# Compressed-branch products of a sparse-attention layer: float32 column tiles in place of full-width split products

## The chip, the cores and the metric

The kernel runs on one core of a Trainium2 chip. The metric is the device time of one execution in microseconds (us). The engines are named as in the profile: PE is the matrix engine (TensorE) and PEld its weight loads, DVE is VectorE, ACT is ScalarE, POOL is GpSimd, and SP issues most DMAs. A name such as L709 is line 709 of the kernel before the change.

## The reference

Two layers on a sequence of 256 tokens of width 1024. Each layer is an adaptive RMS norm, a token mixer, and a gated residual; a final RMS norm follows. Layer 0 is sparse attention with three branches, layer 1 a chunkwise mLSTM. The change lies in layer 0's compressed branch. There, 16 heads in 4 groups (head dimension 64) attend to 15 compressed tokens, made from overlapping blocks of 32 tokens by a small network:

```python
k_cmp = compress_tokens(kv[:, :, 0], ...)      # gelu(flat @ w1 + b1) @ w2 + b2
v_cmp = compress_tokens(kv[:, :, 1], ...)
s_cmp = einsum('bsghd,bcgd->bghsc', q, k_cmp) * scale - slopes * dist_c
p_cmp = masked_probs(s_cmp, dist_c >= 0)
o_cmp = einsum('bghsc,bcgd->bsghd', p_cmp, v_cmp)
...
o = gates[:, :, 0] * o_cmp + gates[:, :, 1] * o_slc + gates[:, :, 2] * o_win
y = o.reshape(B, S, A_WIDTH) * silu(z)
return y @ w_out
```

With 256 tokens the selected and the sliding branch see all earlier keys, so both are plain causal attention over 256 keys of their own.

## The kernel before

**Precision.** Most products are made from split operands: a float32 matrix is written as a rounded part (type float32r, written by ACT, `make_hi`, L165) and the rest (written by DVE, `make_lo`, L170), and three products hi·hi, hi·lo and lo·hi are added up in PSUM. Some smaller products use plain float32 operands. The trace records a float32r product as one matmul and a float32 product as two, each with its weight load.

**Weights.** SP streams blocks of weights of up to 512 KB into ten raw buffers (`_load_one`, L88). A block's successor is loaded when its buffer is released by the split or by the product that reads it raw. Split blocks lie in six pairs of buffers `wh`, `wl`.

**Order.** In layer 0 (`first_phase`, `nsa`, `boundary`) the order of PE, ACT, DVE and SP is the order of the program text, under a manual schedule. In layer 1 of the reference (`layer2` in the code) a planner orders the instructions by its own model of their times, except for a few that are pinned.

**The stretch around the change**, in the program's order, with the names that the steps below use:

- `S(n)` for n = 0 to 7 makes the scores of the selected and the sliding branch for head i = n // 2 of two groups (L959, L963, in PSUM banks 0 to 2); DVE adds the position term and reduces to the minimum (L973); `softmax(n)` is the exp on ACT (L985); `factors(n)` and `scaled(n, j)` scale the probabilities on DVE (L993 to L995, L1002); `T_pair(n, j)` transposes them on PE (L1015, banks 5 and 6) and copies them out on ACT (L1017); `PV(n)` multiplies by the values (L1036, 64-column tiles, bank 7, which it keeps from PV(2i) to PV(2i + 1)).
- `z_steps(n)` are the split products of the gate path (L1662 to L1664, bank 4), in steps of three matmuls; `z_tanh` (ACT, L913) and `z_out` (DVE, L917) read the bank.
- The compressed tokens' second network layer makes `kb` (L679 for the keys, L681 for the values) in bank 3. From it DVE makes `kc` (L683), its rounded part `KcH` (L688) and its rest `KcL` (L689), and the values `Vc` (L694, four instructions). `KcH` and `KcL` have 160 columns for each group, of which 16 hold keys; POOL zeroes the rest (L686, L687). A slice of 128 columns at column 128·g of the flattened tile holds group g's keys at columns 32·g to 32·g + 15, since 160 = 128 + 32, and zeros elsewhere.
- `cmp_scores(i2)` (L709) makes the compressed scores of heads 2·i2 and 2·i2 + 1 in bank 3. Each of its 16 products has 128 columns of weights; the products of the four groups, of KcH and KcL, are added up into one bank half of all 128 partitions, where the zeros keep the groups apart. `Q` holds the rounded part of a query in one half of the partitions and its rest in the other. ACT copies the bank out (L710).
- The program then goes on with S(2), `factors(1)`, `scaled(1, 0)`, the second `cmp_scores`, `scaled(1, 1)`, `softmax` of S(2)'s first half, PV(0), the transposes of the scores `St` (`cmp_tokens(0)`: L724 on PE in bank 3, L725 on DVE), `T_pair(1, 0)`, `cmp_tokens(1)`, a split (L165, L170), and the compressed branch's softmax on DVE and ACT (L738 to L754), interleaved with `z_steps(1)`, S(3) and `T_pair(1, 1)`. Its probabilities come back transposed as `PcT` (L764, L765).
- `compressed(gp)`, at the end of every PV with odd n, adds the compressed branch to bank 7 with two float32 products of 128-column weights (L1028).
- `gate_steps(0, 4)` (float32 products of 32-column tiles, L227) follow in bank 4, after `z_out(1)` has read it.

Of the kernel before, what the change touches and what calls it, by code (L numbers as in the profile page):

```python
# [7 lines left out]
F32 = mybir.dt.float32  # L8
F32R = mybir.dt.float32r
# [3 lines left out]
OP = mybir.AluOpType  # L13
AX = mybir.AxisListType

P = 128
SEQ = 256
# [6 lines left out]
class Kernel:  # L24
# [526 lines left out]
    def nsa(self, acc):  # L551
        nc, t, p1, pc, ident = self.nc, self.t, self.p1, self.pc, self.ident
# [5 lines left out]
        Q = self.Q = []  # L558
# [105 lines left out]
        b = self.bank(3)  # L664
# [9 lines left out]
        self.T_pair(0, 1)  # L674
        self.go(z, 12)
        self.softmax(1)
        kb = self.bank(3)
        for k in range(2):
            nc.tensor.matmul(kb[:, 0:64], self.w2k[:, k].rearrange("p a d -> p (a d)"), hk[:, k], start=(k == 0), stop=(k == 1))  # L679
        for k in range(2):  # L680
            nc.tensor.matmul(kb[:, 64:128], hv[:, k].rearrange("p g s -> p (g s)"), self.w2v[:, k], start=(k == 0), stop=(k == 1), skip_group_check=True)  # L681
        kc = self.T(p1, [P, 4, 16])
        nc.vector.tensor_scalar(kc.rearrange("p g s -> p (g s)"), kb[:, 0:64], 0.5, self.pca[:, 88:89], op0=OP.mult, op1=OP.add)  # L683
        KcH = self.T(p1, [P, 4, 160], F32R, tag="tz", bufs=2)
        KcL = self.T(p1, [P, 4, 160], F32R, tag="tz", bufs=2)
        nc.gpsimd.memset(KcH.bitcast(F32), 0.0)  # L686
        nc.gpsimd.memset(KcL.bitcast(F32), 0.0)  # L687
        nc.vector.tensor_copy(KcH[:, :, 0:16], kc)  # L688
        nc.vector.tensor_sub(KcL[:, :, 0:16], kc, KcH[:, :, 0:16].bitcast(F32))  # L689
        Vc = self.Vc = self.T(p1, [P, 4, 64])  # L690
        nc.gpsimd.memset(Vc, 0.0)
        for g in range(4):
# [5 lines left out]


        St = [self.T(p1, [P, 2, SEQ], tag="y32", bufs=2) for _ in range(2)]  # L700
        KcHf = KcH.rearrange("p g x -> p (g x)")
        KcLf = KcL.rearrange("p g x -> p (g x)")

        def cmp_scores(i2):
            b = self.bank(3)
            for i in (2 * i2, 2 * i2 + 1):
                for g in range(4):
                    for n, kf in enumerate((KcHf, KcLf)):
                        nc.tensor.matmul(b[:, (i % 2) * SEQ : (i % 2) * SEQ + SEQ], kf[:, g * P : g * P + P], Q[i][:, g], start=(g == 0 and n == 0), stop=(g == 3 and n == 1))  # L709
            nc.scalar.activation(St[i2].rearrange("p i k -> p (i k)"), b, AF.Copy)  # L710

        cmp_scores(0)
        self.S(2)
        self.factors(1)
        self.scaled(1, 0)
        cmp_scores(1)
        self.scaled(1, 1)
        self.softmax(2, (0,))
# [300 lines left out]
    def PV(self, n):  # L1019

        nc = self.nc
        i, gp = n // 2, n % 2
        if gp == 0:
            self.ob = self.bank(7)
        o = self.ob[:, gp * SEQ : gp * SEQ + SEQ]

        def compressed(gp):
            nc.tensor.matmul(self.ob[:, gp * SEQ : gp * SEQ + SEQ], self.Vc[:, 2 * gp : 2 * gp + 2].rearrange("p g d -> p (g d)"), self.PcT[:, i], start=False, stop=True, skip_group_check=True)  # L1028

        for br in range(2):  # L1030
            for k in range(2):
                for j in range(2):
                    g = 2 * gp + j
                    oo = o[64 * j : 64 * j + 64, P * k : SEQ]
                    rhs = self.PT[n, j, br][:, 0:256] if k == 0 else self.PT[n, j, br][:, 256:384]
                    nc.tensor.matmul(oo, self.V[br][:, k, 64 * g : 64 * g + 64], rhs, start=(gp == br == k == 0), stop=False, skip_group_check=True, tile_position=(0, 64 * j))  # L1036
        if gp:
            for n in range(2):
                compressed(n)
# [666 lines left out]
```

## Time and profile before

| what | us |
|---|---|
| runs of the kernel before | 457.91, 459.12, 459.18 (median 459.12) |
| profiled execution: span from first to last instruction | 458.1 |
| PE busy | 444.2 (97% of the span) |
| DVE busy | 330.1 (72%) |
| ACT busy | 268.7 (59%) |
| the two `cmp_scores` groups (L709), from the first start | 106.7 to 108.7 and 110.1 to 112.1 |
| `compressed` groups (L1028), first starts | 125.0, 142.1, 165.2, 186.1 |

The profile gives no time of its execution beside the span. The granted clock of PE is 0.995 over the span. DMA moves 95.63 MB at a mean of 209 GB/s; from 103 to 114 us nearly nothing is moved, since all raw buffers are full.

How to read it: "start, length, what" are the first columns of a timeline or chain row; in a timeline a bracket at the end gives the idle time ahead of the row and what ended it. In the chain of waits a row's length is only what it adds to the chain. In a table of waits the numbers are the sum in us, how many times, and the longest. Matmuls are pipelined, so the next one starts before the one ahead of it ends: 0.12 us from start to start for 256 columns, with 0.28 us for each.

### The profile page before, as it was taken

What the parts mean: (1) busy time and instruction counts of PE and PEld (TensorE: products, weight loads), DVE (VectorE), ACT (ScalarE), POOL (GpSimd) and SP (SyncE); (2) the same over time, 40 slices, a digit from 0 to 9 for tenths busy, and PEclk for the clock granted to TensorE, in tenths of its full rate; (3) what the DMA queues carried; (4) which work ended last, traced back from release to release, by engine and by line L of the source; (5) the groups of instructions that cost most, each with busy time, mean ns of one, the idle gap of its engine ahead of it and who ended that gap; (6) DMA issues with size and microseconds to landing.
All of it is one profiled execution on the core that took longest, in us unless ns stands there. A gap on an engine that the chain in (4) does not pass through costs nothing.

```text
span 458.1 us, 8507 instructions
## 1 busy us (share of the span) xinstructions
PE 444.2 (97%) x3120; PEld 377.7 (82%) x3120; DVE 330.1 (72%) x777; ACT 268.7 (59%) x527; POOL 34.8 (8%) x101
## 2 busy tenths in 40 slices
PE   8899999999999999999999999999999999999993
PEld 3799898788948777778899889988888888888883
DVE  3655578886868867587998369688986978455745
ACT  4543377683678777456956686546745556454523
POOL 8820012100000000012000000000000000000000
PEclk9999999999999999999999999999999999999997
DMA  8999999991368899899899998897836699840002
GB/s 275 336 308 296 333 360 292 276 340 48 92 183 279 260 226 298 261 201 172 217 179 110 92 308 286 168 168 225 263 120 221 187 186 280 257 151 1 0 0 92
DMA packets 77596, 95.63 MB, mean 209 GB/s; under 512 B 4540, under 2 KB 56052, under 8 KB 77556
## 3 DMA queue, kind: packets, MB, share of 16 engines
q1 hardware_dynamic: 75828, 92.73, 76.4%
q0 software_dynamic: 1392, 1.58, 1.7%
q10 hardware_dynamic: 336, 0.80, 0.5%
q8 instruction: 24, 0.39, 0.4%
q14 instruction: 16, 0.13, 0.1%
HBM read 93.00 MB, written 1.05 MB: 205 GB/s over the span
## 4 chain that ended last, share of the span: by engine, by line
PE 80%; DMA 7%; DVE 6%; ACT 3%; SPq 3%; issue 1%; ACTq 0%; DVEq 0%
PE bank L547 9%; PE bank L549 9%; PE bank L548 9%; PE bank L1153 8%; PE bank L461 5%; PE bank L870 5%; PE bank L1663 5%; PE bank L1662 5%; PE bank L1664 5%; PE bank L1267 4%; PE bank L227 3%; SPq L88 3%; DMA raw<-in_a_w_in 3%; DMA Q<-in_ada_w 2%; DMA KH<-in_ada_w 2%; PE bank L1036 2%
## 5 line engine op out<-in xcount | busy, mean ns | idle before, releaser
L165 ACT ACTIVATE wh<-raw 128x1024 fp32r<-128x1024 f32 (+5 forms) x126 | 120.9, 977 | 95.1 <-PE bank L549 25.3
L170 DVE TENSOR_TENSOR wl<-raw,wh 128x1024 fp32r<-128x1024 f32 (+5 forms) x126 | 139.7, 1122 | 48.4 <-ACT wh L165 47.6
L547 PE MATMUL bank<-wh,one 128*128 128x512 f32 (+2 forms) x208 | 77.0, 371 | 0.0
L548 PE MATMUL bank<-wl,one 128*128 128x512 f32 (+2 forms) x208 | 76.4, 367 | 0.0
L549 PE MATMUL bank<-wh,one 128*128 128x512 f32 (+2 forms) x208 | 76.3, 368 | 0.0
L1662 PE MATMUL bank<-one,wh 128*128 128x256 f32 x208 | 59.7, 287 | 0.0
L1663 PE MATMUL bank<-one,wh 128*128 128x256 f32 x208 | 59.1, 284 | 0.0
L1664 PE MATMUL bank<-one,wl 128*128 128x256 f32 x208 | 59.1, 284 | 0.0
L547 PEld LDWEIGHTS bank<-wh,one 128*128 128x128 f32 x208 | 39.2, 189 | 7.0 <-issue 0.8
L549 PEld LDWEIGHTS bank<-wh,one 128*128 128x128 f32 x208 | 39.2, 188 | 6.1
L548 PEld LDWEIGHTS bank<-wl,one 128*128 128x128 f32 x208 | 39.2, 189 | 5.9
L1662 PEld LDWEIGHTS bank<-one,wh 128*128 128x128 f32 x208 | 39.8, 191 | 0.7 <-issue 0.4
L1663 PEld LDWEIGHTS bank<-one,wh 128*128 128x128 f32 x208 | 39.8, 192 | 0.1
L1664 PEld LDWEIGHTS bank<-one,wl 128*128 128x128 f32 x208 | 39.8, 191 | 0.0
L461 PE MATMUL bank<-one,wh 128*128 128x256 f32 x224 | 31.5, 286 | 0.2 <-ACT one L425 0.2
L985 ACT ACTIVATE Pr<-Pr,mn 128x128 f32<-128x128 f32 (+1 forms) x64 | 28.2, 448 | 2.4 <-DVE mn L973 2.4
L461 PEld LDWEIGHTS bank<-one,wh 128*128 128x128 f32 x224 | 28.5, 191 | 0.7 <-ACT one L425 0.5
L1153 PE MATMUL bank<-wl,QK 128*128 128x512 f32 (+1 forms) x80 | 28.2, 353 | 0.0
L1153 PE MATMUL bank<-wh,V 128*128 128x512 f32 (+1 forms) x80 | 28.0, 350 | 0.1
L1153 PE MATMUL bank<-wh,QK 128*128 128x512 f32 (+1 forms) x80 | 28.0, 350 | 0.0
L973 DVE CUSTOM_DVE_ANT_0 Pr<-bank,one 128x128 f32<-128x128 f32 (+1 forms) x64 | 18.4, 352 | 5.8 <-PE bank L959 5.7
L1481 DVE SCALAR_TENSOR_TENSOR conv<-bank,one,conv 128x255 f32<-128x255 f32 (+2 forms) x48 | 20.2, 470 | 2.1 <-ACT conv L1476 2.1
(325 smaller groups left out, 769.6 us busy)
## 6 DMA issues: line engine op xcount, KB each, us to landing
raw<-in_b_w_in SPq DMA_DIRECT2D x62, 512.0 KB, 8.3
raw<-in_ada_w SPq DMA_DIRECT2D x34, 512.0 KB, 5.8
raw<-in_b_w_out SPq DMA_DIRECT2D x16, 512.0 KB, 6.4
raw<-in_a_w_in SPq DMA_DIRECT2D x12, 512.0 KB, 7.6
Q<-in_ada_w SPq DMA_DIRECT2D x8, 512.0 KB, 8.2
raw<-in_a_cmp_w SPq DMA_DIRECT2D x8, 512.0 KB, 9.0
raw<-in_a_w_in SPq DMA_DIRECT2D x16, 256.0 KB, 4.2
raw<-in_a_w_out SPq DMA_DIRECT2D x16, 256.0 KB, 5.4
```

What stands on the lines that cost most here:

```text
L165: self.nc.scalar.activation(v(hi), src, AF.Copy)
L170: self.nc.vector.tensor_sub(v(lo), src, v(hi).bitcast(F32))
L461: nc.tensor.matmul(out, w[:, ch * P : ch * P + P], h[:, kk], start=(kk == 0 and m == 0 and ch % 2 == 0), stop=(kk == 7 and m == 2), skip_g ...
L547: nc.tensor.matmul(out, self.hh[:, kk, sl], wh, start=first, stop=False, skip_group_check=True)
L548: nc.tensor.matmul(out, self.hh[:, kk, sl], wl, start=False, stop=False, skip_group_check=True)
L549: nc.tensor.matmul(out, self.hl[:, kk, sl], wh, start=False, stop=last, skip_group_check=True)
L870: nc.tensor.matmul(out, l[:, sl], w[:, c0:c1], start=(k == 0 and m == 0), stop=(k == 7 and m == 2), skip_group_check=True)
L985: self.nc.scalar.activation(v, v, AF.Exp, bias=mn[:, a, br, j : j + 1], scale=-1.0, accum_out=sm[:, a, br, j : j + 1])
L1153: ins = nc.tensor.matmul(out, l[:, sl], w[:, c0:c1], start=(k == 0 and m == 0), stop=(k == N - 1 and m == 2), skip_group_check=True)
L1662: nc.tensor.matmul(out, wh, self.hh[:, kk], start=first, stop=False, skip_group_check=skip)
L1663: nc.tensor.matmul(out, wh, self.hl[:, kk], start=False, stop=False, skip_group_check=skip)
L1664: nc.tensor.matmul(out, wl, self.hh[:, kk], start=False, stop=last, skip_group_check=skip)
```

## The change

Three edits in layer 0.

1. `kb` is made in bank 7 instead of bank 3.
2. `KcH` and `KcL` go. `kc` gets 32 columns for each group, of which DVE writes 16 directly and POOL zeroes all 32 beforehand. A compressed score is now one float32 product for each group and head, with 32 columns of weights, at column tile 32·g of the array; it writes its own 32 partitions of the bank. A call has 8 products instead of 16.
3. `compressed(gp)` makes two float32 products of 64-column weights, one in each column half, instead of one of 128 columns.

```diff
-        kb = self.bank(3)
+        kb = self.bank(7)
...
-        kc = self.T(p1, [P, 4, 16])
-        nc.vector.tensor_scalar(kc.rearrange("p g s -> p (g s)"), kb[:, 0:64], 0.5, self.pca[:, 88:89], op0=OP.mult, op1=OP.add)
-        KcH = self.T(p1, [P, 4, 160], F32R, tag="tz", bufs=2)
-        KcL = self.T(p1, [P, 4, 160], F32R, tag="tz", bufs=2)
-        nc.gpsimd.memset(KcH.bitcast(F32), 0.0)
-        nc.gpsimd.memset(KcL.bitcast(F32), 0.0)
-        nc.vector.tensor_copy(KcH[:, :, 0:16], kc)
-        nc.vector.tensor_sub(KcL[:, :, 0:16], kc, KcH[:, :, 0:16].bitcast(F32))
+        kc = self.T(p1, [P, 4, 32])
+        nc.gpsimd.memset(kc, 0.0)
+        nc.vector.tensor_scalar(kc[:, :, 0:16], kb[:, 0:64].rearrange("p (g s) -> p g s", g=4), 0.5, self.pca[:, 88:89], op0=OP.mult, op1=OP.add)
...
         def cmp_scores(i2):
             b = self.bank(3)
             for i in (2 * i2, 2 * i2 + 1):
                 for g in range(4):
-                    for n, kf in enumerate((KcHf, KcLf)):
-                        nc.tensor.matmul(b[:, (i % 2) * SEQ : (i % 2) * SEQ + SEQ], kf[:, g * P : g * P + P], Q[i][:, g], start=(g == 0 and n == 0), stop=(g == 3 and n == 1))
+                    nc.tensor.matmul(b[32 * g : 32 * g + 32, (i % 2) * SEQ : (i % 2) * SEQ + SEQ], kc[:, g], Q[i][:, g].bitcast(F32), start=True, stop=True, tile_position=(0, 32 * g))
...
         def compressed(gp):
-            nc.tensor.matmul(self.ob[:, gp * SEQ : gp * SEQ + SEQ], self.Vc[:, 2 * gp : 2 * gp + 2].rearrange("p g d -> p (g d)"), self.PcT[:, i], start=False, stop=True, skip_group_check=True)
+            for j in range(2):
+                nc.tensor.matmul(self.ob[64 * j : 64 * j + 64, gp * SEQ : gp * SEQ + SEQ], self.Vc[:, 2 * gp + j], self.PcT[:, i], start=False, stop=True, skip_group_check=True, tile_position=(0, 64 * j))
```

More of the change, by code (lines that the diff above doesn't have):

```diff
@@ L700, in nsa @@
         St = [self.T(p1, [P, 2, SEQ], tag="y32", bufs=2) for _ in range(2)]
-        KcHf = KcH.rearrange("p g x -> p (g x)")
-        KcLf = KcL.rearrange("p g x -> p (g x)")
         def cmp_scores(i2):
```

## The prediction

> **What bounds the kernel now.** I read the page's span and busy shares first, then the busy time by stretches, then PE's waits behind 100 us, and last the chain of waits around the changed lines.
>
> ```profile
> span 458.1 us, 8507 instructions
> PE 444.2 (97%) x3120; PEld 377.7 (82%) x3120; DVE 330.1 (72%) x777; ACT 268.7 (59%) x527; POOL 34.8 (8%) x101
> ```
> ```profile
> core 0: us, PE busy (x) PEld busy (x) DVE busy (x) ACT busy (x) POOL busy (x), PEclk, DMA share, GB/s
> 115.10:127.50 12.40, 12.13 (x103) 10.90 (x101) 11.20 (x41) 8.54 (x28) 0.00 (x0) 1.00 0.29 86
> 137.50:441.00 303.50, 303.45 (x1889) 260.25 (x1890) 227.80 (x475) 184.49 (x332) 4.79 (x16) 1.00 0.78 193
> ```
> ```profile
> PE bank L930 <- ACT adaA L927: 0.7, 1, 0.7
> PE bank L709 <- DVE one L694: 0.5, 1, 0.5
> PE bank L227 <- DVE xT L917: 0.3, 1, 0.3
> ```
>
> PE is the bound: from 137.5 to 441 us it is busy for 303.45 of 303.50 us at clock 1.00. After 100 us only three waits are put down to another engine's work, and two of them lie near the change: L709, the compressed scores, waits 0.5 us for DVE, and L227 waits 0.3 us for L917. The stretch around the change in order of time:
>
> ```profile
> 105.21 0.21 DVE tz L688
> ...
> 105.51 0.23 DVE tz L689
> ...
> 106.33 0.24 DVE one L694
> ...
> 106.71 2.15 PE bank L709 x16
> ...
> 110.27 1.90 PE bank L709 x16
> 112.17 1.45 PE bank L1036 x16
> ...
> 114.21 0.34 PE bank L1015 x3
> ...
> 126.83 0.61 DVE xT L917
> ...
> 127.48 1.92 PE bank L227 x16
> ```
>
> Up to 114.5 us the chain is PE with the two L709 groups in it (2.15 + 1.90); from there to 127.4 it is almost all DVE, which is busy for 11.20 of the 12.40 us from 115.1 to 127.5 (the row above); then PE and, until 137.5, ACT. A shortening in front of 114 us must therefore also move DVE to be worth anything at 127.5.
>
> **The change part by part.** The sum is made against this execution's span of 458.1 us. The page gives no other time for it; the three runs are 457.91, 459.12 and 459.18, so the median stands 1.0 us above the span.
>
> *The bank.* The next rows are of the timelines of PE, DVE and ACT.
>
> ```profile
> 105.98 0.28 PE L1664 MATMUL bank<-one,wl 128*128 128x256 f32 x1
> 106.71 2.15 PE L709 MATMUL bank<-Q,tz 128*128 128x256 f32 x16 [0.45 <-DVE one L694]
> 108.70 0.28 PE L959 MATMUL bank<-KH,Q 128*128 128x256 f32 x1
> ```
> ```profile
> 104.82 0.28 DVE L683 TENSOR_SCALAR one<-bank,one 128x64 f32<-128x64 f32 x1 [1.79 <-PE bank L681]
> 106.92 0.69 DVE L917 SCALAR_TENSOR_TENSOR xT<-zb,bank 128x512 f32<-128x512 f32 x1 [0.36 <-ACT zb L913]
> 109.38 0.29 DVE L973 CUSTOM_DVE_ANT_0 Pr<-bank,one 128x128 f32<-128x128 f32 x1 [1.77 <-PE bank L959]
> ```
> ```profile
> 97.32 0.57 ACT L654 ACTIVATE one<-bank 128x512 f32<-128x512 f32 x1
> ```
>
> The first scores call waits for L694 only because both use bank 3: L694 is the last reader of the products kb. With kb in bank 7 it needs kc alone, ready at 105.10 (104.82 + 0.28). L1664 starts at 105.98 and the z matmuls stand 0.12 apart, so PE goes on at 106.10 and not at 106.71: 0.61 us on PE's path. Bank 7 is free for kb: its previous content is copied out by ACT L654 at 97.32 + 0.57, about 6 us earlier. Its next user, PV(0), comes at 109.5 by the working below, L694 is done 0.44 earlier than now (106.57), at 106.1, so 3.4 us of cover. The removed L688 and L689 (0.44 us) lie on DVE ahead of L694 and of L917, but L917 waits for ACT L913 anyway, so the change on DVE is worth 0 there. If PE were late, they would be worth their 0.4.
>
> *POOL.* Two memsets of 640 columns go, one of 128 columns comes, into a new tile that waits for no reader. They ran at 81.5 and 82.4, more than 20 us ahead of use:
>
> ```profile
> 81.52 0.63 POOL L686 MEMSET tz<- 128x640 f32 x1 [3.74 <-DVE PT L527]
> ```
>
> Nothing waits for them; 0 us. No DMA is added or removed, and no queue of SP or POOL is passed.
>
> *The scores.* Two calls, each 16 fp32r products of 256 columns with 128-column weights, start to next start 1.99 us (106.71 to 108.70). After it each call is 8 float32 products into four 32-column tiles, which the trace records as 16 matmuls, since a float32 product leaves two records. This form stands in L227 (rows of the chain: 128, 128 and 256 columns):
>
> ```profile
> 22.71 0.64 PE bank L227 x16
> ...
> 28.79 1.01 PE bank L227 x32
> ...
> 149.64 1.86 PE bank L227 x32
> ```
>
> The 32 records of 256 columns between full-width work took 1.86 us, so 16 take 0.93 at least. At 128 columns 16 cost 0.64 and 32 cost 1.01; going from 128 to 256 columns adds 0.85 per 32, so 0.43 per 16: 0.64 + 0.43 = 1.07 at most. I take 1.0 from the middle; each call loses 0.99 on PE. The fixed part of these rows (0.27 at zero records) includes the turn between whole array and tiles. The Trainium skill, TensorEngine Tiling (Array Packing), Key Properties, says that changing the tiling mode drains the engine; that speaks against the change, which adds such turns. The rows agree with a small price; without it a call would be 0.85 and the gain 0.15 per call more, with it it is the 1.0 taken.
>
> *What the shortening is worth.* S(2) moves from 108.70 to 107.10 (0.61 + 0.99 = 1.60 earlier), and its first DVE reduction, 0.68 behind it, to 107.78, behind L917's end at 107.61. So DVE gains 1.60. PE then has the second call 0.99 shorter and reaches the transposes of St and T_pair(1,0) 2.6 earlier. There it meets DVE:
>
> ```profile
> 112.25 1.93 DVE L1002 TENSOR_SCALAR Pr<-Pr,f 128x128 f32<-128x128 f32 x8
> 114.25 0.42 DVE L725 TENSOR_TENSOR tz<-bank,one 128x256 f32<-128x256 f32 x1
> 115.42 0.42 DVE L725 TENSOR_TENSOR tz<-bank,one 128x256 f32<-128x256 f32 x1 [0.75 <-PE bank L724]
> 116.11 1.29 DVE L170 TENSOR_TENSOR wl<-raw,wh 128x512 fp32r<-128x512 f32 x2 [0.27 <-ACT wh L165]
> ```
> ```profile
> 114.73 0.66 PE L724 MATMUL bank<-one,y 128*128 128x128 f32 x4
> ...
> 127.48 1.07 PE L227 MATMUL bank<-raw,one 128*32 128x512 f32 x8 [0.27 <-DVE xT L917]
> ```
>
> The second group of L724 needs bank 3 back from the first L725, which ends at 114.67, and starts at 114.73: already tight. The first L725 stands behind the eight L1002, all of which move by 1.60, so PE now waits about 1.0 us at the second L724, and of the second call's 0.99 nothing is left. What is queued behind that wait is z_steps(1). ACT's split L165 stands behind T_pair(1,0)'s copies, which come about 2.5 earlier, so DVE's wait of 0.27 at L170 goes too: DVE gains 1.60 + 0.27 = 1.87 from there, and keeps it up to L917, since little in that stretch is idle. PE itself is free for L227 at 127.21 (127.48 less 0.27), new at 125.6 or before; L917 lets it go at 125.61. Gain there: **1.87 us**. The ACT stretch to 137.5 starts from PE's transposes behind L227 and moves along whole. From 137.5 on PE has no gaps, and the loads go out as slots come free, so what PE gains there it keeps.
>
> *The compressed values.* Each PV with gp = 1 ends with two full-width float32 products, four records:
>
> ```profile
> 90.49 1.88 PE bank L583 x16
> ...
> 140.72 1.45 PE bank L1036 x16
> 142.17 1.06 PE bank L1028 x4
> ```
>
> New are eight records in two 64-column tiles, the form of the PV matmuls ahead of them. L583 is the same form with 256 columns: 0.94 for eight. Or the PV's 1.45 for eight of 256 and eight of 128 columns: 8/12 of it, 0.97. So 0.09 to 0.12 less than 1.06 per PV, up to 0.2 if PV's fixed part (0.17 over the 1.28 that half-rate streaming at 0.107 per record would need) is not paid twice. Taken 0.12. The first of the four lies ahead of the wait for L917 and gives 0; three give **0.36 us**.
>
> Sum: 1.87 + 0.36 = 2.2 us; span 455.9, run median 459.12 - 2.2 = 456.9. Ends: with 1.07 per call, no 0.27 and nothing from the values 1.5 us (457.6); with 0.93, all of both calls and 0.2 on four PVs, 0.61 + 2.12 + 0.8 = 3.5 us (455.6).
>
> **The rivals.**
> *Layer 2 comes out in another order.* Layer 1's order is written out, layer 2's comes from a planner that sees other costs ahead of it. If one split of a block (rows of the raw tiles, fewest, median and longest ns of one) is thereby exposed on PE, it costs its 1.05 on ACT and 1.22 on DVE, 2.27 us:
>
> ```profile
> L165 ACT ACTIVATE wh<-raw x126: 612/1052/1082, 11.2 to 433.4; 128x1024 fp32r<-128x1024 f32 x96, 128x512 fp32r<-128x512 f32 x16, 128x768 fp32r<-128x768 f32 x8, 128x912 fp32r<-128x912 f32 x2
> L170 DVE TENSOR_TENSOR wl<-raw,wh x126: 682/1217/1249, 12.3 to 434.5; 128x1024 fp32r<-128x1024 f32 x96, 128x512 fp32r<-128x512 f32 x16, 128x768 fp32r<-128x768 f32 x8, 128x912 fp32r<-128x912 f32 x2
> ```
>
> Once: 459.2, no change. Twice: 461.4. For it: half of the kernel is planned. Against it: PE had no gap at all there, so blocks lie ready well ahead. No change 0.12, slower 0.05.
>
> *DVE or ACT keeps more of it.* Each small wait that takes the place of the 0.27 (at T_pair(1,0), which needs L1002 0.1 us before PE arrives, or at the exp behind T_pair(1,1)) takes some tenths; four of them leave about 1.2 us, 457.9: no change, 0.10.
>
> *The weight loads do not hide (slower).* 16 loads in front of the matmuls of a call:
>
> ```profile
> L227 PEld LDWEIGHTS bank<-raw,one x192: 106/110/110, 8.2 to 196.9; 128*32 128x32 f32 x192
> ```
>
> 16 x 0.110 + 0.93 = 2.7 us per call against 1.99: 1.4 more for both, less the 0.6 of the bank, 0.8; and in the values eight loads of no less than 0.110 beside 0.94 against 1.06, 0.8 per PV, 2.3 for three. Together 3.1: 462.2. It decides from 2.3 us per call on, where the bank's 0.6 is used up. The L227 row speaks against it: 32 such loads alone would be 3.5 us and the group took 1.86. Chance 0.03. This is the rule of the Trainium skill, TensorE: Matmul & The Clock Gate, Part 3, that a weight load overlaps matmuls in flight only when the row group differs; all these tiles use the same rows. The trace disagrees with it by that row.
>
> **How the numbers follow.** Forecast 0.70, with its own range 455.6 to 457.7; rivals 0.12 + 0.10 for no change and 0.05 + 0.03 for slower. 0.3% of 459.12 is 1.4 us, the size of the runs' own spread (457.91 to 459.18) and about what a measurement tells from no change. Faster 0.70, same 0.22, slower 0.08. The range 455.4 to 458.8 leaves out the slower cases and the upper part of the no-change ones.
>
> **What would show it.** In the changed profile: the first scores group starts 0.1 us behind the last z matmul with no wait for L694's counterpart; each group lasts 0.9 to 1.1 us; S(2) is about 1.6 us earlier against the z matmuls; a new PE wait of about 1 us for the first L725's counterpart at the second group of St transposes; the gate sums start about 1.9 us earlier; eight records behind PV in 0.9 to 1.0 us. The prediction is wrong if a scores group takes over 1.5 us, if the gate sums come less than 1.4 us earlier, or if the stretch from there to the end is longer by over 1 us: then layer 2's order is to be compared.

## The result and the profile after

| | median us | runs |
|---|---|---|
| before | 458.88 | 457.91 to 460.94 |
| changed | 456.71 | 455.94 to 457.54 |

The ratio is 0.9946, with a 95% interval of 0.9932 to 0.9961: 2.2 us shorter. The prediction was 456.9. The profiled execution of the changed kernel has a span of 455.8 us, 2.3 less than the one before.

The new line numbers: L701 are the scores, L951 and L955 S(n), L716 and L717 the transposes of St and DVE's read of them, L994 the scaling, L909 `z_out`, L1021 the compressed values, L1029 PV, L1007 T_pair; L227 and L679 stay. From the timeline of PE of the changed kernel:

```profile
103.53 0.56 PE L679 MATMUL bank<-one,one 128*128 128x64 f32 x4
...
105.72 0.28 PE L1657 MATMUL bank<-one,wl 128*128 128x256 f32 x1
105.93 1.07 PE L701 MATMUL bank<-Q,one 128*32 128x256 f32 x16
106.94 0.39 PE L951 MATMUL bank<-KH,Q 128*128 128x256 f32 x1
107.16 0.28 PE L951 MATMUL bank<-KL,Q 128*128 128x256 f32 x1
107.28 0.29 PE L951 MATMUL bank<-KH,Q 128*128 128x256 f32 x1
...
108.54 1.07 PE L701 MATMUL bank<-Q,one 128*32 128x256 f32 x16
109.54 1.52 PE L1029 MATMUL bank<-PT,one 128*64 128x256 f32 x16
...
112.91 0.66 PE L716 MATMUL bank<-one,y 128*128 128x128 f32 x4 [0.61 <-DVE tz L717]
...
125.34 1.92 PE L227 MATMUL bank<-raw,one 128*32 128x512 f32 x16
```

The first scores group follows the last z matmul after 0.21 us with no wait for DVE. Each group takes 1.01 us to the next start (105.93 to 106.94) where it took 1.99. PE now waits 0.61 us at the second group of St transposes, where it did not wait before. At the gate sums L227 it waits no more. The waits of PE from 100 us to the end:

```profile
PE bank L922 <- ACT adaA L919: 0.7, 1, 0.7
PE bank L716 <- DVE tz L717: 0.6, 1, 0.6
```

The wait of 0.7 us stood there before, too. Ahead of the change PE waits 0.28 us at 96.6 and 1.24 us at 98.3 us; before, it waited 0.85 us at 98.6 us. DVE from 107 us on:

```profile
107.72 0.29 DVE L965 CUSTOM_DVE_ANT_0 Pr<-bank,one 128x128 f32<-128x128 f32 x1 [0.36 <-PE bank L951]
...
110.59 1.92 DVE L994 TENSOR_SCALAR Pr<-Pr,f 128x128 f32<-128x128 f32 x8
112.43 0.41 DVE L717 TENSOR_TENSOR tz<-bank,one 128x256 f32<-128x256 f32 x1
113.60 0.42 DVE L717 TENSOR_TENSOR tz<-bank,one 128x256 f32<-128x256 f32 x1 [0.75 <-PE bank L716]
113.94 1.28 DVE L170 TENSOR_TENSOR wl<-raw,wh 128x512 fp32r<-128x512 f32 x2
```

**A clock that starts at the change.** The start of L679, the first product of the second network layer, moves from one execution to the next, even of one kernel: it is at 103.53 us here and at 104.98 us in a repeat of the changed kernel, at 103.78 us before, and between 102.23 and 105.07 us in the runs below. Distances from it are far steadier. The row of before is

```profile
103.78 0.56 PE L679 MATMUL bank<-one,one 128*128 128x64 f32 x4
```

so the gate sums came 23.70 us behind it (127.48 - 103.78) and now come 21.81 (125.34 - 103.53): 1.89 us earlier. To the end of the span it was 354.3 us and is 352.3: 2.0 us. The repeat gave 21.81 and 352.3 again, at a span of 457.3. The remaining 0.3 us between the two profiled spans is the start of L679, ahead of the change.

### The profile page after: what moved, and what is told of

The parts are those of the page before. It is cut to its first block, busy times and chain, and to the rows that moved or that the text cites. A ratio compares the mean times of both kernels' runs of the same rounds, so it can differ in the third digit from the quotient of the medians.

```text
span 455.8 us, 8536 instructions
## 1 busy us (share of the span) xinstructions
PE 441.3 (97%) x3136; PEld 373.5 (82%) x3136; DVE 329.5 (72%) x775; ACT 268.5 (59%) x527; POOL 33.9 (7%) x100
## 4 chain that ended last, share of the span: by engine, by line
PE 82%; DMA 5%; SPq 4%; DVE 4%; ACT 4%; issue 1%
PE bank L547 9%; PE bank L549 9%; PE bank L548 9%; PE bank L1146 8%; PE bank L1655 6%; PE bank L1656 6%; PE bank L1657 5%; PE bank L862 5%; PE bank L461 4%; PE bank L1260 4%; SPq L88 4%; PE bank L227 3%; PE bank L1007 2%; PE bank L1029 2%; PE bank L1493 2%; DMA Q<-in_ada_w 2%
## 5 line engine op out<-in xcount | busy, mean ns | idle before, releaser
L165 ACT ACTIVATE wh<-raw 128x1024 fp32r<-128x1024 f32 (+5 forms) x126 | 120.9, 977 | 92.8 <-PE bank L549 30.0
L170 DVE TENSOR_TENSOR wl<-raw,wh 128x1024 fp32r<-128x1024 f32 (+5 forms) x126 | 139.7, 1122 | 48.6 <-ACT wh L165 47.7
```

What stands on the lines that cost most here:

```text
L165: self.nc.scalar.activation(v(hi), src, AF.Copy)
L170: self.nc.vector.tensor_sub(v(lo), src, v(hi).bitcast(F32))
```

## The experiments

All distances are from the start of L679 in the same timeline of PE. "To S(2)" ends at its first matmul, "to the gate sums" at the first L227 behind 120 us, "to the end" at the span. The ratios are to the kernel before, in runs on the same chip.

| kernel | to S(2) | to the gate sums | to the end | ratio (95%) |
|---|---|---|---|---|
| before | 4.92 | 23.70 | 354.3 | |
| changed | 3.41 | 21.81 | 352.3 | 0.9946 (0.9932 to 0.9961) |
| the bank alone | 4.23 | 23.01 | 353.7 | 0.9985 (0.9974 to 0.9996) |
| the change less the bank | 3.41 | 21.81 | 352.3 | 0.9944 (0.9929 to 0.9959) |
| the values alone | 4.93 | 23.70 | 354.4 | 1.0005 (0.9987 to 1.0022) |
| the change less the values | 3.41 | 21.81 | 352.3 | 0.9948 (0.9931 to 0.9966) |
| first call twice | 4.27 | 22.68 | 353.1 | 0.9972 (0.9958 to 0.9987) |
| second call twice | 3.41 | 22.27 | 352.7 | 0.9966 (0.9952 to 0.9980) |
| loops exchanged | 3.43 | 21.83 | 352.3 | 0.9942 (0.9928 to 0.9957) |
| eight more on one tile | 6.84 | 25.25 | 355.7 | 1.0018 (0.9999 to 1.0037) |
| full width | 5.59 | 26.04 | 356.5 | 1.0044 (1.0028 to 1.0060) |
| St in bank 1 | 3.41 | 21.40 | 351.8 | 0.9934 (0.9920 to 0.9947) |
| and the gate path early | 3.41 | 20.92 | 351.6 | 0.9927 (0.9903 to 0.9951) |
| changed, a repeat | 3.41 | 21.81 | 352.3 | 0.9953 (0.9931 to 0.9974) |

### One part of the change at a time

**The bank alone**, in the kernel before:

```diff
-        kb = self.bank(3)
+        kb = self.bank(7)
```

> Only the bank of kb is changed (7 for 3); scores and values as before. Distances are from the first key product of the second network layer (L679) to the start of the first gate sums in 32-column tiles: 23.70 us before, 21.81 after. My theory (PE hands the start of S(2) to DVE, DVE hands it on to the gate sums): the first scores group starts 0.6 us earlier, DVE and ACT move along by the same 0.6, so 23.1 us, and a run is 0.6 shorter, about 458.3. Rival (the wait was covered, DVE's chain does not start at S(2)): 23.7 us and no change.

Its timeline of PE:

```profile
103.76 0.56 PE L679 MATMUL bank<-one,one 128*128 128x64 f32 x4
...
106.08 2.07 PE L709 MATMUL bank<-Q,tz 128*128 128x256 f32 x16
...
126.77 1.92 PE L227 MATMUL bank<-raw,one 128*32 128x512 f32 x16 [0.27 <-DVE xT L917]
```

The wait for L694 is gone, the scores start 0.61 us earlier (2.32 behind L679, 2.93 before), S(2) and the gate sums come 0.69 earlier (the group itself takes 1.91 us instead of 1.99), the latter still with the wait of 0.27 us for L917. The theory's 0.6 holds; DVE's chain does hand on what PE gains at S(2).

**The change less the bank**, the changed kernel with `kb` back in bank 3. The expectation speaks of the values as before; the kernel that ran has the values' tiles of the change, which the next two runs show to be worth nothing.

```diff
-        kb = self.bank(7)
+        kb = self.bank(3)
```

> Scores in float32 tiles, values as before, kb in bank 3 as before. My theory: without the two DVE steps for the rounded part and the rest, L694's counterpart ends at about the time of the last z matmul, so the bank edit has nothing left to give once the scores edit is there: L679 to gate sums 21.9 us, time within 0.2 us of the changed kernel. Rival (the edits add up, 0.6 us for the bank and 1.3 for the scores): 22.4 us, and 0.6 us longer than the changed kernel.

```profile
103.21 0.56 PE L679 MATMUL bank<-one,one 128*128 128x64 f32 x4
...
105.62 1.07 PE L701 MATMUL bank<-Q,one 128*32 128x256 f32 x16
```
```profile
104.45 0.91 DVE L689 SCALAR_TENSOR_TENSOR one<-bank,one 32x64 f32<-32x64 f32 x4
```

From L679 to the scores it is 2.41 us, as with bank 7 (2.40). By itself the bank is worth 0.6 us, beside the scores' edit it is worth nothing: without L688 and L689 the last reader of bank 3 (L689 here) is done at 105.36 us (104.45 + 0.91), ahead of the scores' start at 105.62. The parts do not add up, because both remove the same wait.

**The values alone**, and **the change less the values** (each with the one edit of `compressed`, put into the kernel before and taken out of the changed one):

```diff
-            nc.tensor.matmul(self.ob[:, gp * SEQ : gp * SEQ + SEQ], self.Vc[:, 2 * gp : 2 * gp + 2].rearrange("p g d -> p (g d)"), self.PcT[:, i], start=False, stop=True, skip_group_check=True)
+            for j in range(2):
+                nc.tensor.matmul(self.ob[64 * j : 64 * j + 64, gp * SEQ : gp * SEQ + SEQ], self.Vc[:, 2 * gp + j], self.PcT[:, i], start=False, stop=True, skip_group_check=True, tile_position=(0, 64 * j))
```

> Only the compressed values' products are in 64-column tiles. My theory after the result: the turn from tiles to the whole array is only moved from ahead of these products to behind them, so nothing is gained: 6.8 us from the first of them in PV(3) to the next T_pair, as before, and no change of time, 458.9. Rival (the prediction's term): 0.12 to 0.2 us less at each of three places, 6.6 to 6.7 us, and a time 0.36 us shorter.

> The change without its third edit: bank 7 and the scores' tiles, the values as before. My theory: everything that the change brings, L679 to gate sums 21.8 us and the time of the changed kernel, 456.7. Rival (the values bring 0.36 us): 457.1.

The 6.8 us of the expectation are a distance in the chain of waits, from the values' row in PV(3) to the next T_pair: 6.81 us before (142.17 to 148.98), 6.82 with the values alone (143.46 to 150.28). The distance stays, though the group's own row shrinks from the 1.06 us of the kernel before to 0.86:

```profile
143.46 0.86 PE bank L1029 x8
```

The timeline shows where the 0.2 us are, from the start of PV on. First the kernel before, then the values alone (there L1037 is PV, L1029 are the values, L1663 and L1664 the z matmuls):

```profile
140.65 1.52 PE L1036 MATMUL bank<-PT,one 128*64 128x256 f32 x16
142.10 1.13 PE L1028 MATMUL bank<-one,one 128*128 128x256 f32 x4
142.88 0.47 PE L1662 MATMUL bank<-one,wh 128*128 128x256 f32 x1
143.18 0.28 PE L1663 MATMUL bank<-one,wh 128*128 128x256 f32 x1
```
```profile
141.94 1.52 PE L1037 MATMUL bank<-PT,one 128*64 128x256 f32 x16
143.29 1.03 PE L1029 MATMUL bank<-one,one 128*64 128x256 f32 x8
144.25 0.39 PE L1663 MATMUL bank<-one,wh 128*128 128x256 f32 x1
144.48 0.28 PE L1664 MATMUL bank<-one,wh 128*128 128x256 f32 x1
```

| from start to start, us | before | values alone |
|---|---|---|
| PV to the values | 1.45 | 1.35 |
| the values to the first z matmul | 0.78 | 0.96 |
| the first z matmul to the second | 0.30 | 0.23 |
| sum | 2.53 | 2.54 |

The z matmuls' own pace is 0.12. So the four full-width records cost 0.78 and another 0.18 behind them, 0.96 in all, and the eight records in tiles cost 0.96 as well. The turn between tiles and the whole array costs 0.10 us ahead of the values before (1.45 against 1.35) and 0.11 us behind them now (0.23 against 0.12). It is moved and not saved; the third edit is worth 0 us, and the changed kernel without it is as fast.

### What the calls' length is worth

The products of one call are issued twice, the second time over the first. The diff is that of the first call; for the second the range is `1 + i2`.

```diff
         def cmp_scores(i2):
             b = self.bank(3)
+            for _ in range(2 - i2):
                 for i in (2 * i2, 2 * i2 + 1):
```

> The changed kernel with the products of the first scores call issued twice (the second writing over the first). My theory: the call takes 0.85 us more (eight products of 256 columns in four tiles), S(2), DVE and the gate sums come 0.85 later: L679 to gate sums 22.65 us, a run 457.5. Rival (DVE is ahead of PE there, as the wait of 0.36 us at S(2) says that it is not): less than 0.5.

> The changed kernel with the products of the second scores call issued twice. My theory: the same 0.85 us on PE, but PE waits 0.61 us for DVE behind it, so that the second St transposes come only some 0.1 to 0.2 later; ACT's copies and its split come 0.85 later, which puts L170 0.4 later: L679 to gate sums 22.2 us, a run 457.1. Rival 1 (every us of PE counts): 22.65 us. Rival 2 (all of it is covered by the wait): 21.8 us, no change.

First call twice (PE), then second call twice (PE and DVE):

```profile
107.42 1.93 PE L702 MATMUL bank<-Q,one 128*32 128x256 f32 x32
...
115.25 0.66 PE L717 MATMUL bank<-one,y 128*128 128x128 f32 x4 [0.61 <-DVE tz L718]
```
```profile
108.53 1.93 PE L702 MATMUL bank<-Q,one 128*32 128x256 f32 x32
...
125.79 1.92 PE L227 MATMUL bank<-raw,one 128*32 128x512 f32 x16 [0.33 <-DVE xT L910]
```
```profile
114.40 1.29 DVE L170 TENSOR_TENSOR wl<-raw,wh 128x512 fp32r<-128x512 f32 x2 [0.27 <-ACT wh L165]
```

Eight more products cost 0.86 us either way (1.93 against 1.07). In the first call all of it reaches the gate sums (22.68 against 21.81: 0.87), and the wait of 0.61 us behind it stays, since DVE came later by the same. In the second call PE's wait is used up first: DVE's second read of St comes only 0.12 us later (113.71 - 103.52 against 113.60 - 103.53). The 0.46 us that reach the gate sums come by ACT instead: its split L165 starts 0.86 us later behind L679, and DVE waits 0.27 us for it at L170 again, as before the change. Both come out as the theory of DVE's chain had them (22.65 and 22.2); a count of PE's time alone would have made them equal.

### Where a call's shortening comes from

**The loops exchanged**, so that neighbours in the order of issue share a column tile:

```diff
-            for i in (2 * i2, 2 * i2 + 1):
-                for g in range(4):
+            for g in range(4):
+                for i in (2 * i2, 2 * i2 + 1):
```

> The changed kernel with the loops of the scores call exchanged: both heads of a group follow each other on the same column tile, then the next group. Same products, same results, same loads. My theory (the gain comes from four tiles streaming at once): neighbours on one tile run one after the other, a call takes about 2.1 us instead of 1.0, S(2) comes 1.1 later; L679 to gate sums 22.9 us or more, a run 457.8. Rival (a 32-column product is cheap by itself): 1.0 us a call and no change.

```profile
105.80 1.09 PE L701 MATMUL bank<-Q,one 128*32 128x256 f32 x16
106.82 0.39 PE L951 MATMUL bank<-KH,Q 128*128 128x256 f32 x1
```

A call takes 1.02 us and nothing is lost. The expectation of 2.1 us failed. Two readings were left: the tiles work at the same time whatever the order of issue, or a product with 32 columns of weights is cheap by itself. The next two runs tell them apart.

**Eight more products on one tile**, ahead of the first call's:

```diff
+            for i in (0, 1) if i2 == 0 else ():
+                for g in range(4):
+                    nc.tensor.matmul(b[0:32, i * SEQ : i * SEQ + SEQ], kc[:, g], Q[i][:, g].bitcast(F32), start=True, stop=True, tile_position=(0, 0))
```

> The changed kernel; ahead of the first scores call's products stand eight more of the same size, all on column tile 0 (the real ones write over what they leave). It differs from the run with the first call's products issued twice only in that the eight extra ones share one tile. Theory 1 (the gain comes from tiles that stream at the same time, whatever the order of issue): eight products of 0.43 us one after the other, 3.4 us, where eight over four tiles took 0.86; S(2) and the gate sums 3.4 later than in the changed kernel: L679 to gate sums 25.2 us, about 460. Theory 2 (a product with 32 columns of weights is cheap by itself, as the exchanged loops suggested): 0.86 more, 22.7 us.

Its timeline of PE, L701 the extra ones and L704 the real ones:

```profile
104.72 3.42 PE L701 MATMUL bank<-Q,one 128*32 128x256 f32 x15
107.77 0.42 PE L704 MATMUL bank<-Q,one 128*32 128x256 f32 x3
107.98 0.38 PE L701 MATMUL bank<-Q,one 128*32 128x256 f32 x1
108.01 1.21 PE L704 MATMUL bank<-Q,one 128*32 128x256 f32 x13
```

S(2) comes 3.43 us later than in the changed kernel (6.84 against 3.41): 0.43 us for each of eight products, where eight over four tiles cost 0.86 in all. So a product takes 0.43 us and four tiles work on four of them at once. The rows show the order of issue being left as well. The group's first product is issued for tile 0, which is still held by the last record of L701, and the next three are for the other tiles. The rows do not name the tile, but three records of L704 start ahead of that last L701, so they must be those on the other tiles, and they pass the group's first product. This fits the exchanged loops, which cost nothing.

**Full width**: eight float32 products with 128 columns of weights in a call, keys padded with zeros.

```diff
-        kc = self.T(p1, [P, 4, 32])
+        kc = self.T(p1, [P, 4, 160], tag="tz", bufs=2)
...
+            kf = kc.rearrange("p g x -> p (g x)")
             for i in (2 * i2, 2 * i2 + 1):
                 for g in range(4):
-                    nc.tensor.matmul(b[32 * g : 32 * g + 32, (i % 2) * SEQ : (i % 2) * SEQ + SEQ], kc[:, g], Q[i][:, g].bitcast(F32), start=True, stop=True, tile_position=(0, 32 * g))
+                    nc.tensor.matmul(b[:, (i % 2) * SEQ : (i % 2) * SEQ + SEQ], kf[:, g * P : g * P + P], Q[i][:, g].bitcast(F32), start=(g == 0), stop=(g == 3))
```

> The changed kernel with the scores as eight float32 products of full 128-column weights in each call (keys padded with zeros to 160 columns for each group, as KcH was, products of the four groups added up). Theory 1 (tiles at the same time are the gain): a call takes 3.4 to 3.9 us (16 records at the 0.21 to 0.24 of L1028), more than the 2.0 of the split products; two calls put 4.8 us on PE, less the wait for DVE of 0.6 to 0.8: L679 to gate sums about 26 us, a run near 461. Theory 2 (half the products, half the time; the tiles do little): 1 to 1.2 us a call, 22 us.

```profile
104.55 3.61 PE L702 MATMUL bank<-Q,tz 128*128 128x256 f32 x16
107.82 0.47 PE L952 MATMUL bank<-KH,Q 128*128 128x256 f32 x1
```

3.27 us a call (104.55 to 107.82), a little less than the 3.4 expected, and the kernel is slower than before (1.0044, interval 1.0028 to 1.0060). Halving the number of products by going to float32 is a loss by itself; the four tiles at once turn it into a gain.

### Two edits more

The wait of 0.61 us at the second St transposes is one of bank 3 alone, so they were put into bank 1:

```diff
         def cmp_tokens(a):
-            b = self.bank(3)
+            b = self.bank(3 - 2 * a)
```

> The changed kernel with the second group of St transposes in bank 1 instead of bank 3, so that it does not wait for DVE's first read of bank 3. My theory: PE's wait of 0.61 us there goes, and so does DVE's wait of 0.75 us for these transposes; DVE then waits for ACT's split (its first half ends at about 113.5, against L170's start at 113.94), so DVE, and the gate sums with it, gain 0.4 us: L679 to gate sums 21.4 us, a run 456.3. Rival 1 (PE alone counts): 21.2 us, 0.6 shorter. Rival 2 (another wait takes its place): 21.8 us, no change.

DVE and PE with St in bank 1:

```profile
111.16 0.77 DVE L717 TENSOR_TENSOR tz<-bank,one 128x256 f32<-128x256 f32 x2
112.28 1.30 DVE L170 TENSOR_TENSOR wl<-raw,wh 128x512 fp32r<-128x512 f32 x2 [0.34 <-ACT wh L165]
```
```profile
123.66 1.92 PE L227 MATMUL bank<-raw,one 128*32 128x512 f32 x16 [0.41 <-DVE xT L909]
```

Both waits at the St transposes are gone, DVE waits 0.34 us for ACT's split instead, and the gate sums come 0.41 us earlier, as expected. PE waits 0.41 us for L909 now. The last version takes that away too: `z_tanh(1)` directly behind `z_steps(1)`, and `z_out(1)` ahead of `scaled(2, 1)`.

```diff
         self.go(z, 8)
+        self.z_tanh(1)
         self.S(3)
         self.scaled(2, 0)
+        self.z_out(1)
...
         self.scaled(2, 1)
-        self.z_tanh(1)
-        self.z_out(1)
         self.PV(1)
```

> The changed kernel once more, to stand beside the next on the same chip: L679 to gate sums 21.8 us, ratio to before 0.995.

> The kernel with the second St transposes in bank 1, and z_tanh(1) moved to right behind z_steps(1) on ACT, z_out(1) ahead of scaled(2, 1) on DVE, so that the bank of the gate sums is free earlier. My theory: the gate sums wait no longer 0.4 us for DVE's z_out: L679 to gate sums 21.0 us, and since T_pair(2, 1) finds its operand ready, the 0.8 us against the changed kernel last to the end: ratio to the changed kernel of this job 0.998. Rival (DVE then delays T_pair(2, 0) or the exps behind): 21.4 us or a longer way from the gate sums to the second sum over rows (9.80 us in the changed kernel).

The gate sums come at 20.92 us without a wait, but the way from them to the second sum over rows (L922 at its second start) is 10.07 us instead of 9.80, so 0.6 and not 0.9 us are left there, and 0.6 to 0.7 at the end of the span, where 0.8 was expected. The longer way is what the rival had forecast; that DVE is what lengthens it is not shown (see "Open" below). The ratio is 0.9927 (0.9903 to 0.9951) against 0.9953 (0.9931 to 0.9974) for the changed kernel's repeat: the intervals overlap, and only the distances (351.6 against 352.3 us) show the difference plainly. The same holds for St in bank 1 alone.

## Why the prediction was right, and where not

The total came close in part by luck: 2.2 us were forecast, the medians differ by 2.2 and the distance to the end by 2.0 us, but a term of 0.36 us in the sum was worth nothing, and errors in the rest cancel.

- **The wait for the bank** (0.61 us): in the change the scores start 0.53 us earlier behind L679 (2.40 against 2.93). It was credited to bank 7; the run with bank 3 shows that the removed L688 and L689 do it as well. The prediction gave those two 0 us on DVE since L917 waits for ACT anyway. That is right beside bank 7, but it did not see that their removal alone brings L694, the one PE waited for, forward far enough, so that the bank edit is not needed. What is missing from 0.61 is the turn to tiles: the scores follow the last z matmul after 0.21 us and not 0.12.
- **The scores call** (1.0 us, between 0.93 and 1.07): 1.01. The rows of L227 were the right ones. The recorded 0.85 us for a call without the fixed part does not follow from them (1.07 - 0.27 is 0.80); nothing rests on it.
- **S(2) 1.60 us earlier**: 1.51 at its first matmul. DVE's first reduction moved by 1.41 (5.60 us behind L679 before, 109.38 - 103.78; 4.19 now, 107.72 - 103.53), because the first S(2) matmuls behind a tile group are 0.22 us apart instead of 0.12. So DVE misses 0.19 us of the 1.60, which are the two turns: 0.09 ahead of the group (0.21 against 0.12) and 0.10 behind it. The prediction took them to lie inside its 1.0 us, and the measured 1.01 us do not hold them.
- **DVE takes back the second call's shortening**: right in kind. The new wait was 0.61 us and not 1.0. PE reaches T_pair(1, 0), the work ahead of the wait, 2.32 us earlier behind L679 and not 2.6, by the turns, and the second St group comes 1.57 us earlier (112.91 - 103.53 against 114.73 - 103.78). Not all of the second call's shortening is lost, as the run with it issued twice shows: by ACT's split some of it reaches DVE, which the prediction had as its 0.27 us.
- **1.87 us at the gate sums**: 1.89. It is right by errors that cancel. S(2) gave DVE 0.19 less than predicted. The first read of St gave 0.16 more: before, it had waited a little for its transposes (the first L724 group ended at 113.56 + 0.66 = 114.22 and the read started at 114.25, 2.00 us behind the start of L1002; now it is 1.84 us, 112.43 - 110.59). And L170 comes 0.35 us closer to the second read, where 0.27 was counted. Together 1.92, of which 0.03 are lost again up to the gate sums.
- **The values** (0.36 us): 0. This is the step that failed. The price of the tiles was taken from rows that end where a tile group ends (0.94 to 0.97 us; measured 0.96), and the full-width matmul behind it, which pays 0.11 us for the turn, was not in them. The 1.06 us of the old form did hold its turn, so the forecast of 0.12 us for each place was the turn, counted on one side only.
- **PE keeps what it gains**: nearly. From the gate sums to the end it was 330.6 us (458.1 - 127.48) and is 330.5. Inside, two things stand against each other: the ACT stretch up to the second sum over rows is 0.28 shorter, the rest 0.1 longer.
- **The rivals**: a planner that reorders layer 2 did not appear; from the second sum over rows to the end it is 320.6 us before (354.3 - 33.77) and 320.7 after (352.3 - 31.60), and in the last 318 us of both traces PE, ACT, DVE and POOL have the same instructions in the same order, but for the values' records (DMA issues left out). The rival of small waits that eat the gain is out: 1.89 us reach the gate sums, where it would have left 1.2. The rival of weight loads that do not hide is out: 32 loads of 0.110 us (3.5 us) stand in two groups of 1.01 us.

**Open.** The stretch from the gate sums to the second sum over rows is 10.07 us in four kernels (before, bank alone, values alone, gate path early) and 9.79 to 9.81 in the others. The timeline puts it at the second copy of T_pair(2, 1) on ACT, which starts 0.66 us behind the first in the one case and follows it directly in the other. The profile puts the 0.17 us for which ACT is idle ahead of it down to the first copy itself (0.18 in the gate path early); why ACT waits there in some kernels and not in others stays open.

## What to carry to other kernels

Where small float32 products fill only a quarter of the array's columns, four of them in column tiles cost what one costs (0.43 us here); the price of the turn has to be read at the first full-width matmul *behind* the group, not from the group's row. Before adding up the parts of a change, ask which of them remove the same wait. And a gain of 2 us under a run-to-run spread of as much is seen best as a distance from the last instruction ahead of the change.

## What the runs showed of the hardware that was not expected

Products on different column tiles pass each other. An order of issue with neighbours on the same tile cost 1.02 us a call against 1.01, where 2.1 was expected for one behind the other. With eight products queued on tile 0, three records of the group behind them start before the last record of the eight (107.77 against 107.98 us), ahead of a product on tile 0 that was issued before them. The Trainium skill, TensorE: Matmul & The Clock Gate, Part 3, calls the starts of matmuls strictly first in, first out; these rows disagree.
